# A hybrid encoder block on one core: constants in parts, norm rows a step ahead, and the last step of the first projection in pieces

## The chip, the core and the metric

The kernel runs on one core of a Trainium2 chip. The metric is device time in microseconds for one execution; the time before is the median of three runs. Engine names follow the profile: PE is the matrix engine and PEld its weight load, DVE the vector engine, ACT the scalar engine, POOL the general engine, SP the engine whose queue issues most loads.

## What is computed

One layer of a bidirectional hybrid encoder on 256 tokens of width 2,048, in float32. Only the first lines concern the change:

```python
mod = silu(c) @ ada_w + ada_b          # shift_m, scale_m, gate_m, shift_f, scale_f, gate_f
h = rms_norm(x, norm_mix_w) * (1 + scale_m) + shift_m
proj = h @ w_in                        # q, k, v, gates of both branches
...
h_a = bidirectional(mlstm_chunkwise, ...)              # branch A
qkv = silu(centred_depthwise_conv(b_qkv, gdn_conv_w))
o_b = bidirectional(gated_delta_chunkwise, ...)        # branch B
x = x + gate_m * ((g_a * y_a + g_b * y_b) @ w_out)
x = x + gate_f * swiglu(...)
return rms_norm(x, norm_final_w)
```

## The kernel before

**The stages.** The kernel first builds h, transposed: tile `x` holds for each of 16 blocks b of 128 channels a 128x256 piece (channels by tokens). While it builds h it also computes the first 16 column blocks of the projection, the tiles `first[0]` to `first[15]`: gate pre-activations and the first GDN and mLSTM heads. Then a long stage makes the remaining columns in jobs (`z_job`, `a_vo`, `m_job`, `fjob`), woven by hand between the steps of the recurrences; then come the branch outputs, the output projection and the FFN.

**The step of the first stage.** The scale and shift of block b aren't made with a matmul: for 128 channels their columns of `ada_w` come as two 128x2050 rows `ra[0]` and `ra[1]` (2,048 weights and two columns that carry the bias), and DVE multiplies each with `row_c`, which holds silu(c) on every partition, and sums along the row (L523 scale, with the norm's weight from `pk`; L527 shift). Step b therefore loads two such rows and `raw`, 16 weight blocks of 128x128, 3 MB in all, and then runs, in this order:

- DVE L523: the scale sum, into `m2[:, 0]`; L552: x times that sum times `rows`, the reciprocal norms of the tokens, spread over the partitions; L527: the shift sum.
- ACT L555: x plus the shift sum; L556: `hh`, x rounded to float32r. DVE L559: `hl`, what the rounding left over, for the block before.
- PE L561: 16 plain float32 products `first[o] += raw[o] x x[b]`, two instructions each.

In the later stages a float32 product is made as three passes on float32r halves: `wh` is the weight rounded on ACT (L213 in `tjob`), `wl` the rest, subtracted on DVE (L215), and PE adds wh*hh, wh*hl and wl*hh (L234 to L236; L187 to L189 in `fjob`).

**Buffers and queues.** `ra` has five buffers, `raw`, `wh` and `wl` three each. The loads stand on SP's queue, which waits until a buffer is free. Three things set the order on an engine: a planner that takes, by its own estimate of times, the first instruction in program order that is ready; data; and `order(...)`, which pins an instruction behind the one written before it on its engine. What isn't pinned may be moved up.

**After the stage.** `z_job(0, 3)` splits three half chunks of its weights ahead (ACT L213, DVE L215, pinned). `gates` evicts the finished `first` tiles to convolution buffers (ACT L398) and `ev` (L477), makes the gate chain on DVE and ACT (zz at L402, u, gden, its reciprocal at L418, and so on), and runs the depthwise convolutions (ACT L336, DVE L338). The fourth half of z is pinned behind what `gates` has written by then.

**The constants.** At the start, ACT's queue loads c, then `cst` (128x397: a triangle mask, the 128x128 identity `ident`, the sign column and masks) and `pk` (128x402: biases, norm weights, convolution taps and gate constants), each in one transfer.

Of the kernel before, what the change touches and what calls it, by code (L numbers as in the profile page):

```python
# [9 lines left out]
F32 = mybir.dt.float32  # L10
F32R = mybir.dt.float32r
AF = mybir.ActivationFunctionType
ALU = mybir.AluOpType
PSUM = bass.MemoryType.PSUM

P = 128
T = 256
D = 2048
KB = D // P
# [7 lines left out]
N0 = 4 + 3 * GRP  # L27
# [3 lines left out]
PK_NMIX = 96  # L31
PK_NFFN = 112
# [5 lines left out]
PK_N = 402  # L38
# [3 lines left out]
CS_ID = 128  # L42
# [6 lines left out]
CS_N = 397  # L49
# [3 lines left out]
def hybrid_block(ctx: ExitStack, tc: tile.TileContext, xr, nfr, crow, pk_d, cst_d, ada2, ada4, win0, winb, wint, wba, wbb, wo, wgu, wd, out, dbg=None):  # L53
    nc = tc.nc
    V, S, G, PE = nc.vector, nc.scalar, nc.gpsimd, nc.tensor

    def pool(stack, name, bufs=1, **kw):
        return stack.enter_context(tc.tile_pool(name=name, bufs=bufs, **kw))

    cp = pool(ctx, "cp")  # L60
    st = pool(ctx, "st")
# [7 lines left out]
    def big(p, dt, name):  # L69
        return p.tile([P, KB, T], dt, tag="b16", name=name)  # L70

    def order(ins, yes=True):

        return tc.keep_in_program_order(ins) if yes else ins

    def gps(name):
        return g_ps.tile([P, 512], F32, tag="g", name=name)


    row_c = crp.tile([P, D + 2], F32, name="crow")  # L80
    pk = cp.tile([P, PK_N], F32, name="pk")
    cst = cp.tile([P, CS_N], F32, name="cst")
    cp.tile([P, 20], F32, name="edge")
    c1 = st.tile([1, D], F32, tag="raw", bufs=3, name="c1")
    S.dma_start(c1, crow.unsqueeze(0))
    S.dma_start(cst, cst_d)
    S.dma_start(pk, pk_d)
    ident = cst[:, CS_ID : CS_ID + P]
    sgn = cst[:, CS_SGN : CS_SGN + 1]
    ones = cp.tile([P, P], F32, name="ones")  # L90
# [11 lines left out]
    def c_row(g):  # L102
        pc_ = acc_ps.tile([P, 512], F32, tag="acc", name=f"crow{g}")
        order(PE.matmul(pc_, ones[0:1], c1[:, g * 512 : (g + 1) * 512], start=True, stop=True))
        order(S.activation(row_c[:, g * 512 : (g + 1) * 512], pc_, AF.Silu))
# [163 lines left out]
    def fill(n=1):  # L269

        while n and fills:
            if next(fills[0], None):
                n -= 1
            else:
                fills.pop(0)
# [20 lines left out]
    hh = big(bigA, F32R, "hh")  # L296
    hl = big(bigA, F32R, "hl")
# [68 lines left out]
    def z_job(g, early=0):  # L366
        def done(ps):
            szs[g] = evp.tile([P, 2, 512], F32, tag="sz", bufs=1, name=f"sz{g}")
            for t in range(2):
                S.activation(szs[g][:, t], ps[t], AF.Silu)  # L370
        return tjob(f"z{g}", [wint[g, u] for u in range(4)], hh, hl, done, early)
# [121 lines left out]
    with ExitStack() as s0:  # L493
        w0 = pool(s0, "w0")

        x = w0.tile([P, KB, T], F32, name="x")
        ss = w0.tile([P, 2], F32, name="ssx")
        rows = w0.tile([P, T], F32, name="rows")
        xt = []
        for t in range(2):  # L500
            xt.append(w0.tile([P, D + 2], F32, tag="ra", bufs=5, name=f"xt{t}"))
            order(nc.sync.dma_start(xt[t][:, :D], xr[:, t]))

        junk = hl.rearrange("p b t -> p (b t)")
        c_row(0)
        order(S.activation(junk[:, :D], xt[0][:, :D], AF.Square, accum_out=ss[:, 0:1]))
        for g in (1, 2, 3):
            c_row(g)
        order(V.scalar_tensor_tensor(junk[:, D : 2 * D], xt[1][:, :D], 1.0, xt[1][:, :D], ALU.mult, ALU.mult, accum_out=ss[:, 1:2]))
        order(S.activation(ss, ss, AF.Sqrt, bias=epsc, scale=1.0 / D))  # L510

        def loads(b):
            ra = [w0.tile([P, D + 2], F32, tag="ra", bufs=5, name=f"ra{b}_{i}") for i in range(2)]
            raw = st.tile([P, N0, P], F32, tag="raw", bufs=3, name=f"raw0_{b}")
            for i in range(2):
                order(nc.sync.dma_start(ra[i], ada2[b, :, i]))
            order(nc.sync.dma_start(raw, win0[b]))
            return ra, raw

        def scale(b, ra):  # L520
            m2 = w0.tile([P, 2], F32, tag="m2", bufs=3, name=f"m2_{b}")
            f = pk[:, PK_NMIX + b : PK_NMIX + b + 1]
            order(V.scalar_tensor_tensor(ra[0], ra[0], f, row_c, ALU.mult, ALU.mult, accum_out=m2[:, 0:1]))  # L523
            return m2

        def shift(ra, m2):
            order(V.scalar_tensor_tensor(ra[1], ra[1], 1.0, row_c, ALU.mult, ALU.mult, accum_out=m2[:, 1:2]))  # L527

        ra, raw = loads(0)
        m2 = scale(0, ra)  # L530
        order(V.reciprocal(ss, ss))
        dg = w0.tile([P, T], F32, name="dgx")
        for t in range(2):
            order(V.tensor_scalar(dg[:, t * P : (t + 1) * P], ident, ss[:, t : t + 1], None, ALU.mult))
        shift(ra, m2)
        for b2 in range(KB // 2):
            px = gps(f"pxx{b2}")
            for e in range(2):
                for t in range(2):
                    order(PE.transpose(px[:, e * T + t * P : e * T + (t + 1) * P], xt[t][:, (2 * b2 + e) * P : (2 * b2 + e + 1) * P], ident))  # L540
            order(S.activation(x[:, 2 * b2 : 2 * b2 + 2], px.rearrange("p (e t) -> p e t", e=2), AF.Copy))
        prow = acc_ps.tile([P, 512], F32, tag="acc", name="prow")
        order(PE.matmul(prow[:, :T], ones, dg, start=True, stop=True))
        order(S.activation(rows, prow[:, :T], AF.Copy))
        banks = [acc_ps.tile([P, 512], F32, tag="acc", name=f"first{i}") for i in range(4)]
        banks += [gps(f"first{i}") for i in range(4, 8)]
        first = [banks[o // 2][:, (o % 2) * T : (o % 2 + 1) * T] for o in range(N0)]
        for b in range(KB):
            if b:
                ra, raw = loads(b)  # L550
                m2 = scale(b, ra)
            order(V.scalar_tensor_tensor(x[:, b], x[:, b], m2[:, 0:1], rows, ALU.mult, ALU.mult))  # L552
            if b:
                shift(ra, m2)
            order(S.activation(x[:, b], x[:, b], AF.Identity, bias=m2[:, 1:2]))  # L555
            order(S.activation(hh[:, b], x[:, b], AF.Copy))  # L556
            for bb in ((b - 1,) if b < KB - 1 else (b - 1, b)):
                if bb >= 0:
                    order(V.tensor_tensor(hl[:, bb], x[:, bb], hh[:, bb].bitcast(F32), ALU.subtract))  # L559
            for o in range(N0):  # L560
                PE.matmul(  # L561
                    first[o], raw[:, o], x[:, b], start=b == 0 and o % 2 == 0, stop=b == KB - 1 and o % 2 == 1
                )


        zj = z_job(0, 3)
        next(zj)
        fills[:] = [zj] + rest
        zz = w0.tile([P, T], F32, name="zz")
        for i, _ in enumerate(gates(w0, zz, first)):  # L570
            fill(2 if i in (2, 3, 4, 6, 8, 9, 10) else 1)
# [823 lines left out]
    for j in range(FB // 4):  # L1395
# [4 lines left out]
        for e2 in range(2):  # L1400
            px = gps(f"pxf{j}_{e2}")
            for e in range(2):
                f = 2 * e2 + e
                for t in range(2):
                    PE.transpose(px[:, e * T + t * P : e * T + (t + 1) * P], sg[:, t, f * P : (f + 1) * P], ident)
            b = 4 * j + 2 * e2
# [35 lines left out]
    for g in range(4):  # L1442
        c = slice(g * 512, (g + 1) * 512)
# [119 lines left out]
```

## Time and profile before

| | |
|---|---|
| three runs | 1972.22 us median, 1970.23 to 1975.39 |
| the profiled execution | 1972.89 us, of which the span from first to last instruction is 1970.8 us |
| PE busy | 1929.8 us, 98% of the span |
| DVE, ACT, POOL busy | 1405.4, 1025.8, 116.6 us |
| mean granted clock of PE | 0.993 |
| moved by DMA | 485.64 MB, 246 GB/s over the span |
| first stage, PE from its first `first` product | 18.61 to 138.1 us |

A row of the timeline has the start, the duration, engine, line and operation, output and inputs, shapes and count, and in brackets how long the engine was idle before it and who ended that. A row of busy times by stretches has the stretch, its length, busy time and instructions of each engine, the granted clock, the share of time in which the 16 DMA engines were busy, and the rate. A row of a tile's instructions has the count, shortest, median and longest duration in ns, and the first and last start. A row of the DMA issues ends with KB per transfer and the median time from issue to landing.

### The profile page before, as it was taken

How to read it: one execution, taken by the hardware profiler on the slowest of the kernel's cores; microseconds unless marked ns; L12 is line 12 of the kernel's file. 1: busy time of each engine (PE TensorE's matmuls, PEld its weight loads, DVE VectorE, ACT ScalarE, POOL GpSimd, SP SyncE). 2: the span in 40 equal slices, each digit the busy share in tenths (PEclk: the TensorE clock that was granted, in tenths of full speed). 3: DMA queues.
4: the chain of work that ended last, by engine and by line, in shares of the span. 5: the costliest groups of instructions: out<-in, count | busy, mean ns of one | idle time of the engine just before them, and what ended most of it. 6: DMA issues, size and time to landing. Idle time of an engine off the chain costs nothing.

```text
span 1970.8 us, 27090 instructions
## 1 busy us (share of the span) xinstructions
PE 1929.8 (98%) x10418; PEld 1705.2 (87%) x10418; DVE 1405.4 (71%) x2067; ACT 1025.8 (52%) x1551; POOL 116.6 (6%) x211
## 2 busy tenths in 40 slices
PE   8999999999999999999999999999999999999998
PEld 6878889998999899889787888788888888888886
DVE  6779886887788788866577878866665665555554
ACT  3137646765776577565534444644444444444444
POOL 0001210111011101110100000200000000000000
PEclk9999999999999999999899999999999999999999
DMA  9987676667576766686776888576676665565553
GB/s 399 420 349 233 182 255 241 217 221 235 213 219 214 243 209 219 208 293 244 242 296 247 343 301 333 206 255 236 241 268 239 235 239 207 195 214 199 207 199 143
DMA packets 78962, 485.64 MB, mean 246 GB/s; under 512 B 10585, under 2 KB 15969, under 8 KB 24433
## 3 DMA queue, kind: packets, MB, share of 16 engines
q1 hardware_dynamic: 63216, 450.69, 62.6%
q0 software_dynamic: 8160, 17.88, 4.4%
q10 hardware_dynamic: 7458, 15.36, 2.0%
q8 instruction: 81, 1.33, 0.3%
q14 instruction: 47, 0.39, 0.1%
HBM read 467.07 MB, written 16.82 MB: 246 GB/s over the span
## 4 chain that ended last, share of the span: by engine, by line
PE 85%; DVE 6%; DMA 5%; ACT 2%; issue 1%; SPq 0%; ACTq 0%; DVEq 0%
PE acc_gt L234 4%; PE acc_gt L235 4%; PE acc_gt L236 4%; PE acc_up L234 4%; PE acc_up L235 4%; PE acc_up L236 4%; PE acc_d L234 4%; PE acc_d L236 4%; PE acc_d L235 4%; DMA ra<-ada 3%; PE acc_b L187 2%; PE acc_b L189 2%; PE acc_o L236 2%; PE acc_b L188 2%; PE acc_o L234 2%; PE acc_o L235 2%
## 5 line engine op out<-in xcount | busy, mean ns | idle before, releaser
L215 DVE TENSOR_TENSOR wl_d<-raw_d,wh_d 128x1024 fp32r<-128x1024 f32 x88 | 107.7, 1224 | 105.9 <-ACT wh_d L213 105.9
L215 DVE TENSOR_TENSOR wl_up<-raw_up,wh_up 128x1024 fp32r<-128x1024 f32 x88 | 107.6, 1224 | 100.2 <-ACT wh_up L213 100.1
L215 DVE TENSOR_TENSOR wl_gt<-raw_gt,wh_gt 128x1024 fp32r<-128x1024 f32 x88 | 108.1, 1229 | 79.4 <-ACT wh_gt L213 79.4
L187 PE MATMUL acc_b<-hh,wh_b 128*128 128x256 f32 x576 | 162.8, 283 | 0.0
L189 PE MATMUL acc_b<-hh,wl_b 128*128 128x256 f32 x576 | 159.4, 277 | 0.1
L188 PE MATMUL acc_b<-hl,wh_b 128*128 128x256 f32 x576 | 159.1, 276 | 0.0
L213 ACT ACTIVATE wh_d<-raw_d 128x1024 fp32r<-128x1024 f32 x88 | 92.9, 1056 | 126.3 <-PE acc_d L235 118.9
L213 ACT ACTIVATE wh_gt<-raw_gt 128x1024 fp32r<-128x1024 f32 x88 | 92.9, 1056 | 121.2 <-PE acc_gt L235 71.0
L213 ACT ACTIVATE wh_up<-raw_up 128x1024 fp32r<-128x1024 f32 x88 | 92.8, 1056 | 108.1 <-PE acc_up L235 77.1
L124 DVE SCALAR_TENSOR_TENSOR ada<-ada,crow 128x2048 f32<-128x2048 f32 x64 | 145.9, 2283 | 0.0
L234 PE MATMUL acc_gt<-wh_gt,hfh 128*128 128x512 f32 x352 | 135.9, 386 | 0.0
L235 PE MATMUL acc_gt<-wh_gt,hfl 128*128 128x512 f32 x352 | 135.1, 384 | 0.0
L236 PE MATMUL acc_gt<-wl_gt,hfh 128*128 128x512 f32 x352 | 134.2, 381 | 0.0
L234 PE MATMUL acc_up<-wh_up,hfh 128*128 128x512 f32 x352 | 133.4, 379 | 0.0
L235 PE MATMUL acc_up<-wh_up,hfl 128*128 128x512 f32 x352 | 133.4, 379 | 0.0
L236 PE MATMUL acc_up<-wl_up,hfh 128*128 128x512 f32 x352 | 133.4, 379 | 0.0
L234 PE MATMUL acc_d<-wh_d,ffh 128*128 128x512 f32 x344 | 130.5, 379 | 0.0
L235 PE MATMUL acc_d<-wh_d,ffl 128*128 128x512 f32 x344 | 130.5, 379 | 0.0
L236 PE MATMUL acc_d<-wl_d,ffh 128*128 128x512 f32 x344 | 130.4, 379 | 0.0
L561 PE MATMUL first<-x,raw 128*128 128x256 f32 x512 | 114.5, 382 | 7.4 <-ACT x L555 7.0
L561 PEld LDWEIGHTS first<-x,raw 128*128 128x128 f32 x512 | 96.0, 190 | 25.9 <-ACT x L555 12.6
L188 PEld LDWEIGHTS acc_b<-hl,wh_b 128*128 128x128 f32 x576 | 111.3, 193 | 0.1
(382 smaller groups left out, 5262.1 us busy)
## 6 DMA issues: line engine op xcount, KB each, us to landing
ada<-ada SPq DMA_DIRECT2D x64, 1024.0 KB, 6.2
raw_gt<-wgu SPq DMA_DIRECT2D x44, 1024.0 KB, 4.9
raw_up<-wgu SPq DMA_DIRECT2D x44, 1024.0 KB, 4.9
raw_d<-wd SPq DMA_DIRECT2D x44, 1024.0 KB, 4.9
raw_b<-winb SPq DMA_DIRECT2D x36, 1024.0 KB, 5.0
ra<-ada SPq DMA_DIRECT2D x32, 1025.0 KB, 15.6
raw<-win SPq DMA_DIRECT2D x16, 1024.0 KB, 14.5
raw_z<-wint SPq DMA_DIRECT2D x16, 1024.0 KB, 5.2
```

Of the source, the lines that this page charges most:

```text
L124: order(V.scalar_tensor_tensor(raw, raw, 1.0, row_c[:, :D], ALU.mult, ALU.mult, accum_out=mod[:, c : c + 1]))
L187: PE.matmul(o, wh[:, k], woven(hh[:, kk]), start=kk == 0, stop=False)
L188: PE.matmul(o, wh[:, k], woven(hl[:, kk]), start=False, stop=False)
L189: PE.matmul(o, wl[:, k], woven(hh[:, kk]), start=False, stop=kk == KB - 1)
L213: order(S.activation(wh, raws[u][:, k0 : k0 + 2], AF.Copy), early)
L215: order(V.tensor_tensor(wl, raws[u][:, k0 : k0 + 2], wh.bitcast(F32), ALU.subtract), early)
L234: order(PE.matmul(ps[t], xh[:, kk, c], woven(wh[:, k]), start=kk == 0, stop=False), early and steps > 1)
L235: PE.matmul(ps[t], xl[:, kk, c], woven(wh[:, k]), start=False, stop=False)
L236: PE.matmul(ps[t], xh[:, kk, c], woven(wl[:, k]), start=False, stop=kk == last)
L561: PE.matmul(first[o], raw[:, o], x[:, b], start=b == 0 and o % 2 == 0, stop=b == KB - 1 and o % 2 == 1)
```

## The change

All four edits concern the building of h.

- Constants in parts: at the start only the identity's columns of `cst` and the 16 norm weights of `pk` are loaded. `rest_of_constants()`, written after the loop, loads the other columns in four transfers on SP, unpinned.
- Norm rows a step ahead: x[b + 1] is multiplied with `rows` in step b (`spread`), and the scale sum goes into ACT's operation, which already added the shift.
- Last modulation rows in halves: in step 15 each of the two rows is loaded as 1,024 and 1,026 columns and summed as two halves, added by one small operation.
- Last weights in quarters: step 15's `raw` is loaded in four transfers. Blocks 0 to 3 are multiplied as before; blocks 4 to 15 are split into `wh` and `wl`, four blocks at a time, and multiplied as three passes with `hh` and `hl`.

```diff
-    S.dma_start(cst, cst_d)
-    S.dma_start(pk, pk_d)
+    S.dma_start(cst[:, CS_ID : CS_ID + P], cst_d[:, CS_ID : CS_ID + P])
+    S.dma_start(pk[:, PK_NMIX : PK_NFFN], pk_d[:, PK_NMIX : PK_NFFN])
...
+        def spans(b):
+            return (slice(0, 1024), slice(1024, D + 2)) if b == KB - 1 else (slice(0, D + 2),)
...
-                order(nc.sync.dma_start(ra[i], ada2[b, :, i]))
-            order(nc.sync.dma_start(raw, win0[b]))
+                for c in spans(b):
+                    order(nc.sync.dma_start(ra[i][:, c], ada2[b, :, i, c]))
+            n = 4 if b == KB - 1 else N0
+            for o in range(0, N0, n):
+                order(nc.sync.dma_start(raw[:, o : o + n], win0[b, :, o : o + n]))
...
+        def summed(b, rows, f, m):
+            cs = spans(b)
+            for i, c in enumerate(cs):
+                order(V.scalar_tensor_tensor(rows[:, c], rows[:, c], f, row_c[:, c], ALU.mult, ALU.mult, accum_out=m[:, i : i + 1]))
+            if len(cs) > 1:
+                order(V.tensor_tensor(m[:, 0:1], m[:, 0:1], m[:, 1:2], ALU.add))
+
+        def spread(b):
+            order(V.tensor_tensor(x[:, b], x[:, b], rows, ALU.mult))
...
+        def rest_of_constants():
+            for c in (slice(0, CS_ID), slice(CS_ID + P, CS_N)):
+                nc.sync.dma_start(cst[:, c], cst_d[:, c])
+            for c in (slice(0, PK_NMIX), slice(PK_NFFN, PK_N)):
+                nc.sync.dma_start(pk[:, c], pk_d[:, c])
...
-            order(V.scalar_tensor_tensor(x[:, b], x[:, b], m2[:, 0:1], rows, ALU.mult, ALU.mult))
             if b:
-                shift(ra, m2)
-            order(S.activation(x[:, b], x[:, b], AF.Identity, bias=m2[:, 1:2]))
+                summed(b, ra[1], 1.0, m2[:, 1])
+            else:
+                spread(0)
+            order(S.activation(x[:, b], x[:, b], AF.Identity, scale=m2[:, 0, 0:1], bias=m2[:, 1, 0:1]))
             order(S.activation(hh[:, b], x[:, b], AF.Copy))
+            if b < KB - 1:
+                spread(b + 1)
...
-            for o in range(N0):
+            for o in range(N0 if b < KB - 1 else 4):
...
+        wh = [st.tile([P, 8, P], F32R, tag="wh", bufs=3, name=f"wh_first{i}") for i in range(2)]
+        wl = [st.tile([P, 8, P], F32R, tag="wl", bufs=3, name=f"wl_first{i}") for i in range(2)]
+        for o0 in range(4, N0, 4):
+            w = [a[o0 // 8][:, o0 % 8 : o0 % 8 + 4] for a in (wh, wl)]
+            order(S.activation(w[0], raw[:, o0 : o0 + 4], AF.Copy))
+            order(V.tensor_tensor(w[1], raw[:, o0 : o0 + 4], w[0].bitcast(F32), ALU.subtract))
+            for o in range(o0, o0 + 4):
+                PE.matmul(first[o], w[0][:, o - o0], hh[:, KB - 1], start=False, stop=False)
+                PE.matmul(first[o], w[0][:, o - o0], hl[:, KB - 1], start=False, stop=False)
+                PE.matmul(first[o], w[1][:, o - o0], hh[:, KB - 1], start=False, stop=o % 2 == 1)
+        rest_of_constants()
```

More of the change, by code (lines that the diff above doesn't have):

```diff
@@ L515, in loads @@
             for i in range(2):
-                order(nc.sync.dma_start(ra[i], ada2[b, :, i]))
-            order(nc.sync.dma_start(raw, win0[b]))
+                for c in spans(b):
[3 more added lines that the diff above has]
+                order(nc.sync.dma_start(raw[:, o : o + n], win0[b, :, o : o + n]))
             return ra, raw
         def scale(b, ra):
-            m2 = w0.tile([P, 2], F32, tag="m2", bufs=3, name=f"m2_{b}")
-            f = pk[:, PK_NMIX + b : PK_NMIX + b + 1]
-            order(V.scalar_tensor_tensor(ra[0], ra[0], f, row_c, ALU.mult, ALU.mult, accum_out=m2[:, 0:1]))
-            return m2
-        def shift(ra, m2):
-            order(V.scalar_tensor_tensor(ra[1], ra[1], 1.0, row_c, ALU.mult, ALU.mult, accum_out=m2[:, 1:2]))
+            m2 = w0.tile([P, 2, 2], F32, tag="m2", bufs=3, name=f"m2_{b}")
+            summed(b, ra[0], pk[:, PK_NMIX + b : PK_NMIX + b + 1], m2[:, 0])
+            return m2
+        def summed(b, rows, f, m):
[6 more added lines that the diff above has]
+            order(V.tensor_tensor(x[:, b], x[:, b], rows, ALU.mult))
         ra, raw = loads(0)
@@ L534, in hybrid_block @@
             order(V.tensor_scalar(dg[:, t * P : (t + 1) * P], ident, ss[:, t : t + 1], None, ALU.mult))
-        shift(ra, m2)
+        summed(0, ra[1], 1.0, m2[:, 1])
         for b2 in range(KB // 2):
@@ L551, in hybrid_block @@
                 m2 = scale(b, ra)
-            order(V.scalar_tensor_tensor(x[:, b], x[:, b], m2[:, 0:1], rows, ALU.mult, ALU.mult))
             if b:
-                shift(ra, m2)
-            order(S.activation(x[:, b], x[:, b], AF.Identity, bias=m2[:, 1:2]))
+                summed(b, ra[1], 1.0, m2[:, 1])
+            else:
+                spread(0)
+            order(S.activation(x[:, b], x[:, b], AF.Identity, scale=m2[:, 0, 0:1], bias=m2[:, 1, 0:1]))
             order(S.activation(hh[:, b], x[:, b], AF.Copy))
+            if b < KB - 1:
+                spread(b + 1)
             for bb in ((b - 1,) if b < KB - 1 else (b - 1, b)):
```

## The prediction

> **What bounds the kernel now.** I read the page's shares first, then busy time by stretches, then the timeline around the end of the first stage, because the diff touches that stage alone.
>
> ```profile
> span 1970.8 us, 27090 instructions
> PE 1929.8 (98%) x10418; PEld 1705.2 (87%) x10418; DVE 1405.4 (71%) x2067; ACT 1025.8 (52%) x1551; POOL 116.6 (6%) x211
> 63.50:70.97 7.47, 7.17 (x32) 6.00 (x32) 5.40 (x6) 0.86 (x3) 0.00 (x0) 1.00 1.01 421
> 138.10:150.00 11.90, 10.36 (x48) 8.61 (x48) 7.86 (x12) 10.65 (x18) 0.00 (x0) 1.00 0.70 223
> 150.00:1960.00 1810.00, 1790.94 (x9815) 1592.01 (x9814) 1298.10 (x1936) 979.34 (x1465) 114.32 (x201) 0.99 0.67 235
> ```
>
> The stretch rows give length, then busy PE, weight load, DVE, ACT, POOL, clock, DMA share, GB/s. One step of the first stage takes 7.47 us: DMA is full (1.01 at 421 GB/s), PE has 7.17 us of work. So transfers pace the stage, with PE 0.30 us behind. From 150 us on PE is busy 98.9% of 1,810 us: what PE gains by 150 us is kept, what it gains earlier and loses again is not.
>
> ```profile
> 125.22 2.35 DVE L523 SCALAR_TENSOR_TENSOR ra<-ra,pk,crow 128x2050 f32<-128x2050 f32 x1 [2.04 <-DMA ra<-ada]
> 127.62 0.48 DVE L552 SCALAR_TENSOR_TENSOR x<-x,m,rows 128x256 f32<-128x256 f32 x1
> 128.02 2.29 DVE L527 SCALAR_TENSOR_TENSOR ra<-ra,crow 128x2050 f32<-128x2050 f32 x1
> 130.35 0.51 ACT L555 ACTIVATE x<-x,m 128x256 f32<-128x256 f32 x1 [6.52 <-DVE ra L527]
> 130.89 0.42 ACT L556 ACTIVATE hh<-x 128x256 fp32r<-128x256 f32 x1
> 130.91 7.17 PE L561 MATMUL first<-x,raw 128*128 128x256 f32 x32 [0.30 <-ACT x L555]
> 131.34 0.43 DVE L559 TENSOR_TENSOR hl<-x,hh 128x256 fp32r<-128x256 f32 x1 [0.69 <-ACT hh L556]
> 132.14 0.38 ACT L398 ACTIVATE pad<-first 128x256 f32<-128x256 f32 x1 [0.83 <-PE first L561]
> 133.17 2.71 DVE L338 SCALAR_TENSOR_TENSOR cv<-pad,pk,cv 128x256 f32<-128x256 f32 x6 [1.40 <-ACT cv L336]
> 135.79 2.35 DVE L215 TENSOR_TENSOR wl_z<-raw_z,wh_z 128x1024 fp32r<-128x1024 f32 x2
> 137.54 1.05 ACT L213 ACTIVATE wh_z<-raw_z 128x1024 fp32r<-128x1024 f32 x1
> 137.74 0.57 PE L234 MATMUL acc_z<-wh_z,hh 128*128 128x512 f32 x1
> 138.98 1.22 DVE L215 TENSOR_TENSOR wl_z<-raw_z,wh_z 128x1024 fp32r<-128x1024 f32 x1
> 140.12 0.54 DVE L402 TENSOR_SCALAR zz<-first,pk,cst 128x256 f32<-128x256 f32 x1
> 144.59 0.29 DVE L417 TENSOR_SCALAR gden<-u 128x256 f32<-128x256 f32 x1 [3.94 <-ACT u L407]
> 144.92 1.75 DVE L418 RECIPROCAL gden<-gden 128x256 f32<-128x256 f32 x1
> 147.05 1.22 DVE L215 TENSOR_TENSOR wl_z<-raw_z,wh_z 128x1024 fp32r<-128x1024 f32 x1
> 148.32 0.70 PE L236 MATMUL acc_z<-wl_z,hh 128*128 128x512 f32 x2 [1.54 <-DVE wl_z L215]
> ```
>
> This is step 15 and what follows it. PE ends the step, takes the z job at 137.74, and stops at its fourth half, at 148.32, for wl_z. That subtraction is pinned on DVE behind the gate arithmetic, which starts with zz, and zz is pinned behind the third wl_z. From zz to PE's return: 148.32 - 140.12 = 8.2 us. Between 133.17 and zz DVE has no gap: convolution taps and wl_z fill it.
>
> **Start and constants.**
>
> ```profile
> 1.72 0.54 POOL L411 MEMSET tr<- 128x512 f32 x1
> 132.56 0.51 ACT L336 ACTIVATE cv<-pad,pk 128x256 f32<-128x256 f32 x1
> 138.18 0.80 SPq L210 DMA_DIRECT2D raw_z<-wint  x2
> 3.46 11.71 SPq L516 DMA_DIRECT2D ra<-ada  x2
> 12.45 2.35 DVE L523 SCALAR_TENSOR_TENSOR ra<-ra,pk,crow 128x2050 f32<-128x2050 f32 x1 [1.21 <-DMA pk<-pk]
> 18.61 14.08 PE L561 MATMUL first<-x,raw 128*128 128x256 f32 x64 [2.45 <-ACT x L555]
> pk<-pk ACTq DMA_DIRECT2D x1, 201.0 KB, 10.6
> cst<-cst ACTq DMA_DIRECT2D x1, 198.5 KB, 7.9
> ```
>
> The first modulation sum waits 1.21 us for pk; with its 16 columns alone (8 KB) in front the sum starts up to 1.21 us sooner. I cost that at nothing by the end of the stage: the full DMA queue is the cover, and step 15 still waits for its own rows; without that cover it would be at most those 1.21 us.
>
> Of 399.5 KB of constants 72 KB stay in front. The other 327.5 KB are worth 0.335 MB / 421 GB/s = 0.8 us of stream if they move behind it. But the four late transfers are unpinned and wait for no data. POOL's clearing of tr, written after the loop, ran at 1.72 us: the planner lifts what is ready. SP, idle within those 11.71 us, would be given them there, ahead of most loads. So I take 0 and keep -0.8. Loads pinned on SP stand behind nothing new then; if the transfers did stay late, raw_z would be queued behind them, by 0.8 us.
>
> **Step 15 in parts.** Rows applied a step ahead take the L552 operation (0.48, 0.40 to the next) off the path between the two sums; the product moves to step 14's gap on DVE (7.47 - 5.40 us), and ACT's scale rides in an operation it does anyway: nothing added.
>
> ```profile
> 194.64 0.13 DVE L621 TENSOR_TENSOR nn<-sm 128x2 f32<-128x2 f32 x1
> L517 SPq DMA_DIRECT2D raw<-win x3: 327/328/328, 100.8 to 115.7; - x3
> DMA to landing us min/median/max: 14.4/14.5/14.5
> ```
>
> The six 256-column operations at 133.17 take 2.71 us, 0.45 each; 2,050 columns take 2.29: (2.29 - 0.45)/1,794 is 1.03 ns a column and 0.19 fixed, so half a row costs 1.24, and a row in halves 0.19 more than now. A 1 MB row takes 1.05/421 = 2.49 us of stream. Row 0 lands complete at 125.22, row 1 at 127.7, its first half at 126.5. Sum of the last half: 127.7 (DVE is free, its other halves being done at 126.5 and 127.9) or 127.9 + 1.24, plus two small operations of 0.15: 129.5 against 130.35. PE starts 0.56 later, at 130.05; raw's quarters land by 115.7 + 14.5 = 130.2, the first near 128.3. Gain 0.85 us.
>
> ```profile
> L187 PE MATMUL acc_a<-hh,wh_a x16: 272/275/275, 296.7 to 301.7; 128*128 128x256 f32 x16
> L189 PE MATMUL acc_a<-hh,wl_a x16: 275/275/275, 296.9 to 302.0; 128*128 128x256 f32 x16
> 151.70 0.61 ACT L605 ACTIVATE kqh<-kq 128x512 fp32r<-128x512 f32 x1
> 175.86 0.66 DVE L606 TENSOR_TENSOR kql<-kq,kqh 128x512 fp32r<-128x512 f32 x1
> ```
>
> A plain block now costs PE (137.74 - 130.91)/16 = 0.43 us. A split one costs three matmuls at 5.3 us/47 = 0.113, that is 0.34. Four plain and twelve split: 1.7 + 4.06 = 5.8 us against 6.83. PE would reach z at 135.8, 1.9 us sooner. The splits cost ACT 3 x 0.61 and DVE 3 x 0.66, at these rows' prices, right where ACT now idles 0.83 and DVE 0.69 + 1.40 us. ACT: hh ends near 130.45 (0.85 sooner than 131.31), plus 1.7 with slight overlap is 132.1, and the first eviction is as late as now (132.14). DVE: the last wl ends near 132.9, before cv (133.1). So the gain on the gate side is used up by the splits: cv, wl_z and zz stay where they are to 0.1 us.
>
> **Waits that are added.** The step's two pairs of wh and wl take two of three buffers of each kind. The first wh_z has the third; the second waits on ACT for PE's blocks 4 to 7 (131.8 + 1.35 = 133.1), the third for PE's last (135.8). ACT works in order, so an eviction that the planner puts behind the third wh_z comes at 136.9 instead of 132.14, and the taps on DVE with it. That costs PE nothing by itself, since it needs no tap before 150 us; but up to four evictions (0.38 each) and two copies (0.51) would then stand on ACT before the gate's own operations: 2.5 us off the 1.9 gained in that order, +0.6. Against this, raw_z's third transfer, issued at 138.18 as the stage's last weights come free, can go at 132.9; nothing waited for it.
>
> **The sum.** PE arrives at z 1.9 us sooner, but its fourth half waits for zz + 8.2 us. If the order on DVE stays, PE returns at 148.2-148.3: the 1.9 us turn into a longer stall, result 0. If the planner puts all three wl_z ahead of the taps, zz can start when the third is done. Its wh_z needs a buffer that PE gives back at 135.8: 135.9 + 1.05 + 1.22 = 138.2, so 1.9 us sooner, with the taps in DVE's gap of 3.94 us behind zz. Bounds -1.9 and +0.6. I take -0.8, between the kept order (0) and the best one, since wl_z is written ahead of the taps and goes first whenever both are ready. The profiled execution took 1972.89 us (span 1970.8), 0.67 above the median 1972.22; a difference of -0.8 gives 1971.4 from the median.
>
> **Rivals.** *More, smaller transfers slow the stream.*
>
> ```profile
> outT<-x SPq DMA_DIRECT2D x7, 256.0 KB, 2.4
> raw_gt<-wgu SPq DMA_DIRECT2D x44, 1024.0 KB, 4.9
> ```
>
> 256 KB land in 2.4 us and 1 MB in 4.9, so (4.9 - 2.4)/768 KB leaves 1.6 us that do not depend on size. There are nine more transfers (six for two constants, eight for three in step 15). If each occupied the queue for its 1.6 us, the stage would end 14 us later: 1986, slower by 0.7%. It decides as soon as more than about 3.7 of the nine aren't overlapped (5.9 us). Against it: three 1 MB transfers take 7.47 us in steady state, 2.49 each, well under 4.9, so the fixed part overlaps when queued. Chance 5%. [...]
>
> *Everything is kept.* Reordered gates (-1.9) and constants truly late (-0.8), and no stall left at the fourth half (PE idle 1.54 there now): -4.2 us, 1968.0. Still within 0.3%. 10%.
>
> *The later order changes.* The planner's times shift by a microsecond, and unpinned work may change places over the remaining 1,800 us, either way. PE idles 19 us there (1,810 - 1,791), so a third more or less of this is 6 us: 1966 or 1978. 15% that it passes the bound downward (the first stage's change points that way), 8% upward.
>
> *The change doesn't do what it says:* constants that aren't late are inside the forecast.
>
> **How the numbers follow.** Differences below 0.3% (5.9 us) can't be told from none. The forecast with its bounds holds 62%, everything kept 10%: within 0.3% together 72%. Faster by more: 15%. Slower by more: 5% from transfers, 8% from order, 13%. The range leaves out the far ends of the last two rivals and reaches to 1965 and 1978.
>
> **What would show it.** Right: first L523 no longer ended by pk; the late constants issued before 20 us; the last L555 near 129.5; z on PE near 135.8; zz near 140 and a stall of some 3.5 us at the fourth wl_z. Wrong: steps longer than 7.47 us, zz near 138, constants issued after 120 us, or a difference that grows after 150 us.

## The result

The changed kernel is slower: 1982.82 us median of 7 runs (1981.28 to 1985.30) against 1972.27 us of 7 runs of the kernel before (1970.23 to 1977.56). The ratio is 1.0048, 95% interval 1.0039 to 1.0057; the medians lie 10.5 us apart. The forecast was 1971.4, "within 0.3%", range 1965 to 1978.

The same views as in the prediction, now of the changed kernel. Up to L500 its lines have the old numbers; L534 holds both modulation sums, L574 the scale and shift on ACT, L590 and L591 the splits of the last weights, L593 to L595 the three passes, L562 and L564 the late constants. The page's shares first, then busy time by stretches, with the same columns:

```profile
span 1979.7 us, 27170 instructions
PE 1930.5 (98%) x10430; PEld 1704.8 (86%) x10430; DVE 1407.1 (71%) x2076; ACT 1033.4 (52%) x1557; POOL 116.6 (6%) x211
```

```profile
63.50:70.97 7.47, 7.12 (x33) 5.96 (x32) 5.34 (x6) 1.02 (x2) 0.00 (x0) 1.00 1.01 419
138.10:150.00 11.90, 8.47 (x38) 7.10 (x38) 5.81 (x8) 11.09 (x18) 0.00 (x0) 1.00 0.37 129
```

PE has as much work as before (1930.5 against 1929.8 us) in a span that is 8.9 us longer, and a step of the first stage still takes 7.47 us. The difference is waiting, and the stretch from 138 to 150 shows where it begins: PE has 8.47 us of work there instead of 10.36, while ACT is fuller than before (11.09 against 10.65 of 11.90). The timeline of that place:

```profile
123.44 1.61 SPq L562 DMA_DIRECT2D cst<-cst  x2
125.99 1.61 SPq L564 DMA_DIRECT2D pk<-pk  x2
128.00 0.33 SPq L210 DMA_DIRECT2D raw_z<-wint  x1
128.75 0.60 ACT L574 ACTIVATE x<-x,m 128x256 f32<-128x256 f32 x1 [5.61 <-DVE m L536]
129.70 1.65 ACT L590 ACTIVATE wh_first<-raw 128x512 fp32r<-128x512 f32 x3
130.34 1.90 DVE L591 TENSOR_TENSOR wl_first<-raw,wh_first 128x512 fp32r<-128x512 f32 x3
135.21 0.38 ACT L477 ACTIVATE ev<-first 128x256 f32<-128x256 f32 x1 [1.59 <-PE first L595]
135.92 0.38 ACT L477 ACTIVATE ev<-first 128x256 f32<-128x256 f32 x1 [0.32 <-PE first L595]
136.20 1.99 ACT L213 ACTIVATE wh_z<-raw_z 128x1024 fp32r<-128x1024 f32 x2
137.30 0.48 PE L234 MATMUL acc_z<-wh_z,hh 128*128 128x512 f32 x1 [1.42 <-ACT wh_z L213]
140.76 1.06 ACT L213 ACTIVATE wh_z<-raw_z 128x1024 fp32r<-128x1024 f32 x1 [0.23 <-PE acc_z L235]
141.71 0.54 DVE L402 TENSOR_SCALAR zz<-first,pk,cst 128x256 f32<-128x256 f32 x1
141.84 1.28 ACT L341 ACT_TABLE_LOAD   x1
143.13 0.42 ACT L341 ACTIVATE kq<-cv 128x256 f32<-128x256 f32 x1
143.45 0.40 ACT L406 ACTIVATE u<-zz 128x256 f32<-128x256 f32 x1
146.89 0.42 ACT L407 ACTIVATE u<-u 128x256 f32<-128x256 f32 x1
147.34 0.29 DVE L417 TENSOR_SCALAR gden<-u 128x256 f32<-128x256 f32 x1 [5.09 <-ACT u L407]
149.80 2.35 DVE L215 TENSOR_TENSOR wl_z<-raw_z,wh_z 128x1024 fp32r<-128x1024 f32 x2
151.07 0.85 PE L236 MATMUL acc_z<-wl_z,hh 128*128 128x512 f32 x2 [4.09 <-DVE wl_z L215]
```

ACT in the trace of before, of which the prediction shows only the third wh_z:

```profile
134.21 2.01 ACT L213 ACTIVATE wh_z<-raw_z 128x1024 fp32r<-128x1024 f32 x2
140.69 0.42 ACT L406 ACTIVATE u<-zz 128x256 f32<-128x256 f32 x1 [0.87 <-DVE zz L402]
144.14 0.42 ACT L407 ACTIVATE u<-u 128x256 f32<-128x256 f32 x1
144.56 1.04 ACT L213 ACTIVATE wh_z<-raw_z 128x1024 fp32r<-128x1024 f32 x1
```

And the stretch right behind PE's wait in the changed kernel:

```profile
152.00:154.00 2.00, 2.00 (x6) 1.53 (x6) 2.00 (x5) 0.86 (x2) 0.00 (x0) 0.50 0.95 274
```

Read from the top. The late constants are issued at 123.4 to 127.6, in front of raw_z, whose first load goes at 128.00 instead of 123.18. The scale and shift of step 15 end sooner, as worked out (128.75 against 130.35). But the first wh_z on ACT starts at 136.20 (before 134.21), and zz is 1.6 us later. That isn't raw_z's landing: it landed 5.9 us after its issue, at 133.9, and ACT stood idle for 1.59 us until 135.21. The first wh_z stands behind two evictions (ev, L477), and these wait for the last products of step 15. Then ACT takes the fourth wh_z, a table load (the load of a function table, 1.28 us) and a silu (L341) before u, so u starts 1.74 us behind the start of zz instead of 0.57. From there on the chain takes as long as before: PE returns 7.62 us behind u's start (before 7.63). So gden comes at 147.34 instead of 144.59, and PE returns to z's fourth half at 151.07 instead of 148.32, after a wait of 4.09 us (before 1.54). In the stretch behind that wait the granted clock is 0.50.

A second wait stands 28 us later, for the decays (alpha) of the first head:

```profile
165.24 0.33 SPq L210 DMA_DIRECT2D raw_v<-wint  x1
165.44 0.70 POOL L442 DMA_DIRECT2D alpha_d<-s  x1 [162.59 <-ACT s L441]
170.68 1.49 POOL L317 DMA_DIRECT2D al<-alpha_d  x2 [4.34 <-DMA alpha_d<-s]
171.44 0.48 PE L236 MATMUL acc_v<-wl_v,hh 128*128 128x512 f32 x1 [0.71 <-DVE wl_v L215]
177.38 0.69 DVE L627 TENSOR_TENSOR_SCAN dec<-al,cst 128x256 f32<-128x256 f32 x1 [4.47 <-DMA al<-alpha_d]
179.24 0.48 PE L236 MATMUL acc_v<-wl_v,hh 128*128 128x512 f32 x1 [2.36 <-DVE wl_v L215]
```

The same places in the trace of before:

```profile
166.44 1.49 POOL L317 DMA_DIRECT2D al<-alpha_d  x2 [1.40 <-DMA alpha_d<-s]
168.21 0.33 SPq L210 DMA_DIRECT2D raw_v<-wint  x1
174.76 0.48 PE L236 MATMUL acc_v<-wl_v,hh 128*128 128x512 f32 x1 [0.70 <-DVE wl_v L215]
```

In the changed kernel a 1 MB load goes out 0.20 us ahead of the small store of alpha, and POOL waits 4.34 us for the store instead of 1.40. The scan that needs alpha holds DVE, wl_v stands behind it there, and PE waits.

Added up: 2.75 at the return to z (1.59 for the later zz, 1.16 for the later u), 1.7 for one record of half clock that lasts 3.41 us, and 0.71 + 2.36 - 0.70 = 2.37 in the waits for wl_v: 6.8 us. Counted back from the last matmul, so that the same work is compared, PE is 7.0 us behind the kernel before at 240 us and 8.6 behind at the end. This count, "the lag at 240", is used below, since it leaves out what the rest of the program does. It comes from one trace of each kernel, and a second trace of the kernel before (e17 below) is itself 1.3 us behind the first at 240, so a lag of 1 or 2 us can't be told from none.

### The profile page after: what moved, and what is told of

The parts are those of the page before. It is cut to its first block, busy times and chain, and to the rows that moved or that the text cites. A ratio compares the mean times of both kernels' runs of the same rounds, so it can differ in the third digit from the quotient of the medians.

```text
span 1979.7 us, 27170 instructions
## 1 busy us (share of the span) xinstructions
PE 1930.5 (98%) x10430; PEld 1704.8 (86%) x10430; DVE 1407.1 (71%) x2076; ACT 1033.4 (52%) x1557; POOL 116.6 (6%) x211
## 4 chain that ended last, share of the span: by engine, by line
PE 80%; DVE 8%; DMA 7%; ACT 3%; issue 2%; POOL 0%; SPq 0%; DVEq 0%; POOLq 0%; ACTq 0%
PE acc_gt L234 4%; PE acc_gt L235 4%; PE acc_gt L236 4%; DMA ra<-ada 4%; PE acc_up L235 4%; PE acc_up L236 4%; PE acc_up L234 4%; PE acc_d L234 4%; PE acc_d L236 4%; PE acc_d L235 4%; PE acc_b L187 2%; PE acc_b L189 2%; PE acc_b L188 2%; PE acc_o L236 2%; PE acc_o L234 2%; PE acc_o L235 2%
## 5 line engine op out<-in xcount | busy, mean ns | idle before, releaser
L582 PE MATMUL first<-x,raw 128*128 128x256 f32 x488 | 109.1, 382 | 5.9 <-ACT x L574 5.9
L582 PEld LDWEIGHTS first<-x,raw 128*128 128x128 f32 x488 | 91.6, 190 | 23.4 <-ACT x L574 11.5
```

What stands on the lines that cost most here:

```text
L582: PE.matmul(first[o], raw[:, o], x[:, b], start=b == 0 and o % 2 == 0, stop=b == KB - 1 and o % 2 == 1)
```

## The experiments

Two theories at the start. **Q, the queue:** the late constants delay raw_z on SP, and all else follows. **S, the splits:** the three splits on ACT and DVE delay the gate chain. After the first four runs S became **G, the order:** each edit shifts the planner's estimates, and what it then puts on ACT ahead of u decides how long PE waits; the rest follows from that wait, half clock behind it included (G's clock part: in the changed kernel a wait of 4.09 us and a granted clock of 0.50 behind it). The traces show the order that came out; why the planner chose it, they don't show.

**Parts taken out, and parts alone.** Part 1 is the constants, 2 the rows a step ahead, 3 the sums in halves, 4 the quarters with three passes.

```diff
 e1_consts_whole: the kernel after
+    S.dma_start(cst, cst_d); S.dma_start(pk, pk_d)     # instead of the columns
-        rest_of_constants()
 e2_consts_only: the kernel before
+    S.dma_start(cst[:, CS_ID : CS_ID + P], ...); S.dma_start(pk[:, PK_NMIX : PK_NFFN], ...)
+        rest_of_constants()                             # behind the loop
 e3_no_passes: the kernel after; e4_passes_only: the kernel before, with these lines
-            for o in range(N0 if b < KB - 1 else 4):
+            for o in range(N0):
-        for o0 in range(4, N0, 4): ...                  # splits and three passes
-            n = 4 if b == KB - 1 else N0
+            n = N0
```

> The changed kernel with both constants loaded whole at the start again (part one undone), all else kept. Theory Q (queue): the four late transfers stand on SP ahead of raw_z and move its first issue from 123.2 to 128.0; that puts wh_z behind other ACT work, zz 1.6 us later and makes PE's wait for the fourth wl_z 4.09 us, long enough for the granted clock to halve. Without them raw_z goes at 123-124, zz starts at 140.3 or sooner, the wait is 3 us or less, the clock stays at 1.00, and the time is 1971 to 1975. Theory S (splits): the three wh and wl of step 15 delay the gate chain whatever the queue does; zz stays at 141.5 or later, the wait at 4 us, the time at 1981 to 1984.

> The kernel before with part one alone (constants in parts, the rest loaded late). Theory Q: raw_z is issued 2 to 5 us later than 123.2, zz 1 to 2 us later than 140.1, PE's wait at the fourth wl_z 2.5 to 3.5 us; 1973 to 1978. Theory S: no change, 1972.

> The changed kernel without the last weights in quarters as three passes (one transfer, sixteen plain products). Theory Q: raw_z is still behind the late transfers, by less since there are three transfers fewer; PE reaches z near 137 and waits about 3 us; 1973 to 1978. Theory S: zz back to 140 or sooner, 1970 to 1972.

> The kernel before with part four alone (last weights in quarters as three passes). Theory Q: raw_z at 123-125, zz near 140, PE reaches z 1.0 us sooner and waits that much longer (2.5 us), clock at 1.00; 1971 to 1973. Theory S: zz 1.5 us later, the wait near 4 us, the clock halved for one window; 1978 to 1983.

> The kernel before with only the norm rows applied a step ahead and the last modulation rows summed in halves (constants and passes as before). [...] Theory A (the loss adds up edit by edit): after is +10.5, constants alone +2.4, passes alone +4.4, so the rows alone would be about +3.7, 1977.

Later two more, which split part 4:

```diff
 e15_quarters_plain: the kernel after, quarters loaded, no splits
-            for o in range(N0 if b < KB - 1 else 4):
+            for o in range(N0):
-        for o0 in range(4, N0, 4): ...
 e16_passes_whole: the kernel after, splits kept, one load
-            n = 4 if b == KB - 1 else N0
+            n = N0
```

> The kernel after with the last weights still loaded in four transfers, but multiplied plainly: no splits on ACT and DVE, no three passes. If the splits shift the gate chain's order (theory G): as without the whole of that part (1975.5 in e3), 1974 to 1977, fourth part of z back on TensorE by 148.5. If the four transfers with their waits shift it: 1981 to 1984.

> The kernel after with splits and three passes, but the last weights in one transfer. Theory G: the splits stay, so the stall at the fourth part stays near 4 us, with the window of half clock behind it: 1981 to 1984. If the transfers are the cause: 1974 to 1977. In the order that comes out, one load of a function table (1.28 us) that after has ahead of u is gone, so 1979 to 1982 would speak for the order, not for the splits' own time.

| kernel | parts | median us | ratio to before, interval | zz, u behind it (us) | PE back in z, its wait there (us) | half clock behind it | lag at 240 |
|---|---|---|---|---|---|---|---|
| before | | 1972.27 | | 140.12, 0.57 | 148.32, 1.54 | no | |
| after | 1 2 3 4 | 1982.82 | 1.0048 [1.0039, 1.0057] | 141.71, 1.74 | 151.07, 4.09 | yes | 7.0 |
| e1 | 2 3 4 | 1983.34 | 1.0055 [1.0034, 1.0076] | 140.44, 2.01 | 150.07, 4.09 | yes | 7.4 |
| e2 | 1 | 1975.60 | 1.0011 [1.0002, 1.0020] | 140.44, 0.95 | 149.01, 2.35 | yes | 3.2 |
| e3 | 1 2 3 | 1975.46 | 1.0011 [1.0001, 1.0021] | 139.79, 0.95 | 148.36, 2.35 | no | 1.2 |
| e4 | 4 | 1977.62 | 1.0023 [1.0008, 1.0038] | 140.54, 0.58 | 148.75, 1.54 | no | 1.8 |
| e5 | 2 3 | 1974.49 | 1.0008 [0.9999, 1.0018] | 139.63, 0.57 | 147.84, 1.54 | no | 0.0 |
| e15 | 1 2 3, quarters | 1975.40 | 1.0007 [0.9997, 1.0017] | 141.21, 0.58 | 149.42, 2.63 | no | 1.7 |
| e16 | 1 2 3, passes | 1977.62 | 1.0020 [1.0010, 1.0029] | 139.94, 0.73 | 148.29, 2.36 | yes | 2.3 |

The fifth column has the start of zz, and how long after it u starts on ACT. Each ratio is to runs of the kernel before in the same session, whose medians lie between 1972.27 and 1973.69 us.

Q falls as the whole cause: with the constants back at the start (e1) raw_z goes out at 124.11 and zz comes at 140.44 (before 123.18 and 140.12), and the time is no better. Nor do the late constants alone hold raw_z up: in e2 it goes out at 122.53, and in e4, with the quarters but early constants, at 123.13. Late constants and quarters together do it (128.00 in the changed kernel, 127.75 in e15), and in these two the first wh_z stands behind the evictions and zz is 1.1 to 1.6 us late. Nor do the parts add up (theory A of the expectation for e5): alone they cost 0.08% to 0.23%, without part 4 the rest costs 0.11%, all together 0.48%. In part 4 either half alone loses less than both: without the splits 0.07%, without the quarters 0.20%.

What goes with PE's return is the start of u on ACT. In all nine rows PE is back 7.62 to 7.64 us behind it. Where u starts as soon as zz is done (before, e4, e5, e15) that is 0.57 or 0.58 us behind zz's start; in e15 the fourth wh_z stands ahead of u, but is done before zz. Where the fourth wh_z stands ahead of u and waits longer for PE to give a buffer back (e1, e2, e3, e16) it is 0.73 to 2.01, and with the silu and its table load there too (after) 1.74. The wait in z also depends on when PE gets there, so it is the poorer measure: in e15 it is 2.63 us with u as close to zz as before.

In e1:

```profile
141.49 1.06 ACT L213 ACTIVATE wh_z<-raw_z 128x1024 fp32r<-128x1024 f32 x1 [1.68 <-PE acc_z L235]
142.45 0.40 ACT L406 ACTIVATE u<-zz 128x256 f32<-128x256 f32 x1
145.89 0.42 ACT L407 ACTIVATE u<-u 128x256 f32<-128x256 f32 x1
150.07 0.70 PE L236 MATMUL acc_z<-wl_z,hh 128*128 128x512 f32 x2 [4.09 <-DVE wl_z L215]
```

ACT stands still for 1.68 us, waiting for PE to give back a wh buffer, with u's first operation behind it, though zz was there at 140.44 + 0.54. In e4 (part 4 alone) the same operation stands behind u, and u is as close to zz as before.

Many expectations missed. Q gave the times of e2 and e3, but in e2 neither raw_z nor zz is late as it said, and e1 and e4 were slower than it said. S gave e1's time, but had zz there at 141.5 or later. e5, at 1974.49, came just above the 1970 to 1974 that G gave, far from A's 1977. e15's time is that of G, but PE was back in z at 149.42 and not by 148.5; e16, with a wait of 2.36 us and 1977.62 us, fits none of its three cases.

**The order by itself.** e11 writes the gates' sigmoid in another place; the work is the same, and the order that comes out has u ahead of the fourth wh_z and of the first silu, as in the kernel before, with two table loads fewer than the changed kernel up to 200 us (nine, as many as before). The first wh_z stays behind the evictions there. e6 writes z's fourth half ahead of the gates' arithmetic; e14 is e6 once more. e7 fills the wait with matmuls whose result nothing uses.

```diff
 e11_gate_order: the kernel after
-        S.activation(tr[0:32, 0], zz[0:32], AF.Sigmoid)         # behind ea
+        S.activation(tr[0:32, 0], zz[0:32], AF.Sigmoid)         # behind u * den
 e6_fourth_first, e14: the kernel after
-            fill(2 if i in (2, 3, 4, 6, 8, 9, 10) else 1)
+            fill((2, 2, 1, 1, 2, 1, 2, 1, 2, 2, 2)[i] if i < 11 else 1)
 e7_warm: the kernel after, behind z's third half
+                for i in range(16):
+                    order(PE.matmul(wp, xh[:, 0, 0:P], xh[:, 0:2]..., start=True, stop=True))
```

> The kernel after with the sigmoid's line written behind the product with gden. The order that comes out has the same work, but u ahead of the fourth wh_z and of the first silu, as before the change, and two table loads of 1.28 us fewer. Theory G: the fourth wl_z comes 2.5 to 4 us earlier, the stall of 4.09 us falls to 0.5 to 2, no half clock follows: 1975 to 1978. If the loss lies in the late transfers or in the splits themselves: 1981 to 1984.

> The kernel after with the fourth part of z written ahead of the gate arithmetic, so that wl_z of that part is made before gden on DVE. Theory G: the stall of 4.09 us before the fourth part goes and one of about 1.2 to 1.5 us comes at the fifth; no half clock follows; 1976 to 1979, 4 to 7 us under after. If the stall is only a mark of something later (theory L: the alpha store and the order behind it set the end), the time stays at 1981 to 1984.

> The kernel after with 16 idle 128x512 matmuls behind the third part of z, which fill the stall of 4.09 us and are used by nothing. Theory G with its clock part: TensorE is never idle long there, no window of half clock at 151.5, and the 2.1 us that it cost come back: 1980 to 1981. If the clock's dip there doesn't come from the stall, it stays, and the time is 1982.8 or a little more.

e11: 1978.53 us, ratio 1.0031 [1.0020, 1.0043]; PE waits 1.12 and 1.54 us in z, there is no half clock, alpha doesn't collide, and the lag at 240 is 1.7 instead of 7.0. zz is nearly as late as in the changed kernel (141.53), but u starts 0.57 us behind it. In these two traces the order between zz and u, with what followed from it, therefore makes 5.3 of the 7.0 us; the rest is about what the late zz costs (1.4). The time was expected at 1975 to 1978 and lies just above, because e11 loses 3.8 us more after 240. So of the 10.5 us between the medians e11 gives back 4.3, and what the later stages add is not explained.

e7: 1979.36 us, 1.0032 [1.0017, 1.0047], 0.6 us under G's range. The busy time by stretches in e7, where the changed kernel has 0.50:

```profile
146.00:151.00 5.00, 4.59 (x21) 3.46 (x20) 3.73 (x5) 4.96 (x8) 0.00 (x0) 1.00 0.00 0
152.00:154.00 2.00, 2.00 (x11) 1.76 (x10) 2.00 (x6) 1.78 (x3) 0.00 (x0) 1.00 0.87 279
```

wl_z comes from DVE as late as in the changed kernel (149.66 against 149.80), but with PE busy the clock stays at 1.00: the wait is what halves it. The lag at 240 falls by 4.2, more than the 1.7 of the clock, since alpha's store doesn't collide here. So it doesn't price the clock alone.

e6 missed: 1982.48 us, 1.0049 [1.0032, 1.0066], where G expected 1976 to 1979. In its trace the wait of 4.09 us is gone as expected (1.50 remain, at the fifth part), there is no half clock, and at 176 us PE is 0.7 us ahead of the kernel before. Then alpha's collision comes again (POOL waits 3.74 us for the store, PE 2.88 and 1.18 for wl_v), and the lag at 240 is 3.4: all of it arises there. But it loses more at 594 us, where its order of work is the old one:

```profile
593.98 0.44 PE L642 MATMUL vps<-cst,vf 128*128 128x128 f32 x2 [2.70 <-ACT vf L341]
```

> The kernel of e6 once more, for a second trace of the same program. In e6 TensorE was 3.4 us behind the kernel before from 240 to 480 us, and lost 4.5 us more at 594 (a stall of 2.81 us before vps against 1.57, and half clock behind it), where its order of work is that of before and one transfer landed 1.2 us later. If that is the chance of the moment (theory C): the stall there is 1.1 to 1.7 in this trace and the span 4 us shorter, 1978. If it belongs to the program (theory P): 2.8 again, span 1982.

> The kernel before once more, for a second trace. In the first, TensorE stalled 1.57 us before vps at 587.9, in e6 and its second trace 2.81 and 3.05 us at the same place in the work. If that belongs to each program (theory P): 1.4 to 1.7 again. If it is chance (theory C): any value from 1.1 to 3.1.

The two expectations count these waits 0.11 us longer than the rows do. e14 took 1987.18 us and e17 1971.60, one run each. The row is the same place in the second trace of e6, then in the second and the first of the kernel before:

```profile
596.70 0.44 PE L642 MATMUL vps<-cst,vf 128*128 128x128 f32 x2 [2.94 <-ACT vf L341]
```

```profile
589.07 0.44 PE L609 MATMUL vps<-cst,vf 128*128 128x128 f32 x2 [1.35 <-ACT vf L341]
```

```profile
587.85 0.44 PE L609 MATMUL vps<-cst,vf 128*128 128x128 f32 x2 [1.46 <-ACT vf L341]
```

So in these four traces the wait goes with the program, not with the single execution (theory P). It is 2.4 to 2.9 in e4, e7 and e9 too, and 1.0 to 1.5 in all the others. In e6 ACT waits 1.96 us for a raw_b load there, in before 0.73. Why a load issued at the same place in the order lands 1.2 us later in some programs was not found. The two traces of the kernel before also show how far single traces reach: the second is 1.9 us behind the first at 710 us and 1.3 ahead at the end. Differences of that size after 240 us are not explained here.

**Alpha's store.** e9 issues it from ACT's queue instead of POOL's.

```diff
 e9_alpha_act: the kernel after
-            G.dma_start(alpha_d.rearrange("d h t -> (d h) t"), s2[32:64])
+            S.dma_start(alpha_d.rearrange("d h t -> (d h) t"), s2[32:64])
```

> The kernel after with the store of alpha issued from ACT's queue instead of GpSimd's. In after it landed 4.34 us after its issue (1.40 in before) beside the load of raw_v. If the queue is the cause: it lands in about 1.4 us, al comes 2 to 3 us earlier, the stall of 2.36 us at 179 goes, 1980 to 1981. If it is the channels that the load fills, whatever queue it comes from: it lands after 4 us as before and the time stays at 1982 to 1984.

1982.65 us, 1.0052 [1.0036, 1.0067]: no gain in the median of four runs (1980.35 to 1985.66). The store landed in 1.5 us, and PE's wait near 179 is gone (1.45 at 173.4 instead). But it doesn't tell queue from load, because here the store went out at 166.34, 0.23 us ahead of raw_v's load, not behind it. And the trace, which is of the slowest of the four runs, lost elsewhere. The order on ACT is that of the changed kernel, but the clock fell already behind PE's wait of 1.42 us at the start of z, which the changed kernel has too:

```profile
138.50:141.91 3.41, 3.41 (x10) 2.69 (x9) 2.45 (x3) 1.21 (x2) 0.00 (x0) 0.50 0.70 209
```

So PE gave the wh buffer back later, the fourth wh_z came at 142.09 and PE was back in z at 152.39, 1.3 us later than in the changed kernel. Inconclusive.

**Versions that could beat both.** If u sets PE's return, the two table loads (1.28 us each, at 141.12 and 142.85) that stand between u's two operations in the kernel before are in the way. e10 pins the sigmoid behind u; e12 does it in e5.

```diff
 e10_sigmoid_behind: the kernel before; e12_rows_sigmoid_behind: e5
-        S.activation(tr[0:32, 0], zz[0:32], AF.Sigmoid)
+        order(S.activation(tr[0:32, 0], zz[0:32], AF.Sigmoid))
```

> The kernel before with one thing moved: ACT takes the gates' sigmoid (tr) after the exponential (u) instead of ahead of it; in before the two function tables it needs (1.28 us each, at 141.12 and 142.85) stand in a row before u, which gden and behind it the fourth wl_z wait for. Theory G (the gate chain on ACT and DVE sets TensorE's return at 148.3): the fourth wh_z comes in ahead of u, so u starts 0.5 to 1.7 us earlier, the stall of 1.69 us shrinks to 0 to 1.2 and the time goes down by 0.5 to 1.7: 1971 to 1972.3. Theory L (what is gained here is taken back by later transfers that don't move): 1972 to 1974, the same.

> The same move in the kernel with the norm rows ahead and the sums in halves (e5). Theory G: e5 was 0.5 us ahead at the return of TensorE, with this 1 to 2.2 us: 1970.5 to 1972. Theory L: 1972 to 1975, as e5.

```profile
140.64 1.04 ACT L213 ACTIVATE wh_z<-raw_z 128x1024 fp32r<-128x1024 f32 x1
141.70 1.28 ACT L407 ACT_TABLE_LOAD   x1
142.99 0.42 ACT L407 ACTIVATE u<-u 128x256 f32<-128x256 f32 x1
147.17 0.70 PE L236 MATMUL acc_z<-wl_z,hh 128*128 128x512 f32 x2 [0.84 <-DVE wl_z L215]
```

In e12 (rows above) u comes 1.15 us sooner than in before and PE waits 0.84. The times: e10 1971.80 us, 0.9993 [0.9984, 1.0003], no difference that can be told; e12 1971.81 us, 0.9991 [0.9982, 0.9999], against 1973.32 us of before in the same session: 1.5 us, at the edge of what can be told. It beats both kernels, by little. The traces show why it isn't more: of the 1.2 us that e12 is ahead at 176 us, 0.1 is left at 240, and in e5 0.5 becomes 0.0. ACT in e5, and the same place in before:

```profile
225.11 1.06 ACT L213 ACTIVATE wh_v<-raw_v 128x1024 fp32r<-128x1024 f32 x1 [2.33 <-DMA raw_v<-wint]
226.08 0.61 ACT L622 ACTIVATE sqkq<-kq 128x512 f32<-128x512 f32 x1
```

```profile
224.86 1.06 ACT L213 ACTIVATE wh_v<-raw_v 128x1024 fp32r<-128x1024 f32 x1 [1.55 <-DMA raw_v<-wint]
```

The load of raw_v lands no sooner in e5, sqkq stands behind it on ACT, and PE waits for sqkq there. On this reading a gain meets the next load that is just in time and ends, while a loss has nothing to take it back: theory L, as far as 240 us. It is argued and not shown. The second trace of the kernel before (e17) has the same wait at this place (2.35 us on ACT, 0.28 on PE), without any gain ahead of it.

## Why the prediction was wrong

- **Stage and start: right, but for one mark.** Steps stay at 7.47 us, and the 14 us of the rival of small transfers didn't come: PE ends step 15 at 135.9, before at 137.7. The first sum starts at 11.29 instead of 12.45 and that is worth nothing later, as said; the part of pk still ends its wait (0.68 us), so the mark "no longer ended by pk" was wrong.
- **Late constants: wrong.** They were said to be lifted ahead of most loads; they went out at 123.4 to 127.6. raw_z's first load came 4.8 us later, not the 0.8 of the other case. e1 shows that the loss doesn't need this: without it the time is the same, by another order on ACT.
- **Step 15: right in its parts, wrong at its end.** L574 came at 128.75 (said 129.5), and scaling cost 0.60 instead of 0.51, not "nothing added". The splits and three passes ran near their prices, and PE ended the step at 135.9 (said 135.8). But it then waited 1.42 us for wh_z, and began z at 137.30. The prediction had evictions that might stand behind wh_z on ACT; here wh_z stood behind evictions.
- **The step that failed: on the gate side "cv, wl_z and zz stay where they are to 0.1 us", and PE's return at zz + 8.2 us, bounds -1.9 and +0.6.** zz came at 141.71 (1.6 later, with the first wh_z behind the evictions) and the return at zz + 9.4: +2.75 us. The 8.2 was taken as a fixed length. Of it 7.6 is fixed, from u's start on, but the 0.57 from zz to u holds only while nothing else stands on ACT between them. The prediction saw that ACT works in order and that wh_z waits for buffers (in e1 u stood behind such a wait of 1.68 us, with zz there); it put that price on the evictions, and let the fourth wh_z and the silu with its table load stay behind u. In the changed kernel both moved ahead, in e1 the fourth wh_z alone, and e11, which puts both back, takes the lag from 7.0 to 1.7.
- **A price that was missing: the clock.** A stall of "some 3.5 us at the fourth wl_z" was forecast as harmless, because PE's work was waiting for it anyway. The stall came (4.09) and half clock for 3.41 us behind it, 1.7 us; with PE kept busy in e7 it didn't.
- **The later order.** It was a rival at 8%, up to 1978, without a place. It has one: alpha's store beside a raw_v load, with 2.4 us more of PE's waits for wl_v. The rest to the end, some 1.6 us in this trace, is as large as two traces of one kernel differ, and stays open.
- Each failure went to the same side. The range to 1978 took the rivals one at a time; here a late chain, its clock and the collision behind it came together.

## What to carry to other kernels

Price an edit at the end of a stage by the chain that releases the bound engine, with every instruction that stands or could stand on its engines in between: a planner that sees times shift by a microsecond may put a table load or an instruction that waits for a buffer ahead of the one that matters, so pin that one. A wait of the matrix engine is charged twice when the clock falls behind it (here 4.09 us of wait, then 1.7 us lost at half clock). And a gain may last only as far as the next transfer that lands just in time (of the 1.2 us that e12 was ahead at 176 us, 0.1 was left at 240; that the transfer did it is argued and not shown).

## What the runs showed of the hardware

- In the records of before and after the clock falls in whole pieces: each stretch at half clock (0.50) lasts 3.41 us, or two or three times that (6.83, 10.24), but for the one that runs past the end of the program, and all of them start on one grid of 3.41 us through an execution (378.6, 955.4 and 1027.1 us in before lie 169 and 21 pieces apart). Waits of 4.08 or 4.09 us in z were followed by one in each of three traces (after, e1, e9); waits of 2.35 to 2.63 in two of four (e2 and e16, not e3 and e15); those of 1.54 in none; that of 1.42 at the start of z in e9 alone.
- In these traces, what tells the cases apart is how the wait falls on the grid. The piece ahead of half clock in e2, then the two pieces that share the wait in e15:

```profile
146.72:150.13 3.41, 1.12 (x5) 1.02 (x6) 3.38 (x5) 3.41 (x7) 0.00 (x0) 1.00 0.09 17
```

```profile
144.68:148.09 3.41, 2.11 (x10) 1.51 (x8) 2.33 (x3) 3.38 (x6) 0.00 (x0) 1.00 0.00 0
148.09:151.51 3.42, 2.09 (x10) 1.85 (x11) 3.42 (x4) 3.42 (x8) 0.00 (x0) 1.00 0.27 57
```

PE is busy for 1.12 us of the piece in e2, 1.27 in e16 and 1.47 ahead of the early half clock in e9; in e3 and e15 no piece has less than 2.09. From 125 to 200 us, in all traces, every piece with 1.47 us or less was followed by half clock, and none with more: the nearest has 1.50 (after, 175.38 to 178.79). By these numbers, as an estimate, a wait of 4.09 us leaves one piece with at most 3.41 - 4.09 / 2 = 1.37 wherever it falls, a wait of 2.35 only if it lies mostly in one. This holds for z and the stage behind it; later other things count too, since at 378.6 us before lost the clock behind a piece with 2.24 us of work on PE and a wait of 1.17.
- ACT with a scale that is read from a tile took 0.60 us for 128x256 (L574 in after, 16 times), without it 0.51 (L555 in before, 16 times).
- A small store (32 KB) that went out 0.20 us behind a 1 MB load kept its reader waiting 4.34 us (4.33 in e1, also 0.20 behind; 3.74 in e6, 0.66 behind; 1.30 in e7, 3.65 behind); with the load 4 us later, 1.40; 0.23 us ahead of the load, it landed in 1.5. Whether the load alone makes it was not tested.
